# Storing the prompt's result of a convolution and S5 step by token phase: 64 outermost rows in place of 2

## The chip, the cores and the metric

The kernel runs on one core of one Trainium2 chip. The metric is the device time of one execution in microseconds (us), and of several runs the median. Before the change three runs took 2135.16, 2134.79 and 2128.93 us, median 2134.79 us.

## The reference, cut to what matters

The reference is one inference step of a two-layer trunk in float32: a short gated convolution layer and an S5 (diagonal state space) layer with a GLU, each with a residual, then a final RMSNorm. The prompt has 256 tokens, the sample batch 8, the model width is 2048 and the inner width 4096. What the change touches is the end alone: the normalised prompt rows are written out.

```python
def rmsnorm(x, g):
    xf = x.astype(jnp.float32)
    xf = xf * lax.rsqrt(jnp.mean(xf * xf, axis=-1, keepdims=True) + EPS)
    return (xf * g.astype(jnp.float32)).astype(x.dtype)
...
    y_prompt = rmsnorm(xp, final_norm)
    y_sample = rmsnorm(xs, final_norm)
```

y_prompt is 1 x 256 x 2048 float32, 2.10 MB; y_sample is 8 rows of 8 KB, 64 KB.

## The kernel before

Nearly the whole kernel is one stream of weights. SyncE (SP in the profile) loads 1 MB blocks of weights from DRAM (line 187), ScalarE and VectorE split each into two parts (lines 196 and 205), and TensorE multiplies the parts with the activations (lines 230 to 233), for the two input projections, the GLU and the two output projections in turn. The order of the work on each engine is the order in which the code records it; `Stream.go` (line 100) walks the weight blocks and puts the other work between them. All transfers of the kernel's end are issued by SP, one behind the other (`wq` is SyncE).

Tokens are kept in the order of their phase: token t = 4c + s stands at position s*64 + c, with s the phase (0 to 3) and c the chunk (0 to 63). So after the last output projection (`ssm_out`, line 1130), when results are transposed back to one token per partition, half h of the result (h = 0 or 1) has phase 2h in its partitions 0 to 63 and phase 2h + 1 in its partitions 64 to 127. The tile `o01` (a view of `yb`) holds both halves, 128 partitions x 2 x 2048.

When the weight stream has ended, the tail runs: sums of squares per token (lines 1128 and 1219 to 1222), the reciprocal root (`rstd_from`, lines 267 to 273), five scalings of pieces of `o01` (line 1229 on VectorE, line 1231 on ScalarE), and then five stores of these pieces (line 1233), in the order of the pieces, each behind a wait for the engine that scaled it. The sample's rows are scaled and stored last (lines 1234 and 1235). Line 1260 is the program's end: SP waits there for the last transfers, and the engines meet.

The view `yp` gives the result in DRAM by phase: index (phase, chunk, column), where neighbouring chunks of one phase lie four tokens apart, 32 KB. A store of half h takes two phases of it, so the access pattern in DRAM is 2 x 64 x columns, and that on the chip is 128 partitions x columns.

Each transfer that SP issues signals its landing on one of eight semaphores, which are used in turn; a transfer waits before its issue until the one eight places earlier, which had the same semaphore, has landed, unless something else has shown that already.

Of the kernel before, what the change touches and what calls it, by code (L numbers as in the profile page):

```python
# [23 lines left out]
NCH = 64  # L24
NP = LC * NCH
T = NP + NS
# [12 lines left out]


class Stream:
    """Slots of the weight stream, and what is issued between them: processes that yield a wait in slots (int), a wait
    for the time of a transfer (Lag) or the vector time they have taken (float). Side processes share a budget of vector
    time per slot."""

    def __init__(self):
        self.slots, self.now, self.t = [], 0, 0.0
# [28 lines left out]
                        again = True  # L76

    def fill(self, fn):
        """Independent vector work, issued where a chain of dependent instructions would wait, or at the slot's end."""
        self.fills.append(fn)  # L80

    def pop_fill(self):
# [42 lines left out]
def tile_hybrid_conv_s5_step(  # L125
# [7 lines left out]
    PE, V, A, P = nc.tensor, nc.vector, nc.scalar, nc.gpsimd  # L133
    mult, add, sub = ALU.mult, ALU.add, ALU.subtract
    wq, mq = nc.sync, nc.sync
# [3 lines left out]
    psm = ctx.enter_context(tc.tile_pool(name="psm", bufs=4, space=PSUM))  # L139
    pss = ctx.enter_context(tc.tile_pool(name="pss", bufs=2, space=PSUM))  # L140

# [1 line left out]
    ident = const.tile([128, 128], F32, name="ident")  # L143
    make_identity(nc, ident)
    ones = const.tile([128, 128], F32, name="ones")
# [19 lines left out]
    cp_d = dram.tile([128, G, GS], F32, name="cp_d")  # L165
    h0_d = dram.tile([128, NS, G], F32, name="h0_d")

# [1 line left out]
    wraw = ctx.enter_context(tc.tile_pool(name="wraw", bufs=3))  # L169
    wsp = ctx.enter_context(tc.tile_pool(name="wsp", bufs=4))  # L170
    s0p = ctx.enter_context(tc.tile_pool(name="s0p", bufs=1))
# [1 line left out]
    run = Stream()  # L173
    spawn, side = run.spawn, run.side

# [1 line left out]
    raws, whs, wls = {}, {}, {}  # L177

    def load_raw(i, parts=1, between=lambda: None):
# [116 lines left out]
    cs = cc.tile([128, KI, NS], F32, name="cs")  # L296
    wk = enter("convwk", 2)

    # ================= tokens to feature-major =================
    # token order s*64 + c for t = 4c + s, then the samples  # L300
    st_p = tc.tile_pool(name="start", bufs=1)
    sp = st_p.__enter__()
    xin = [sp.tile([128, D], F32, name=f"xin{i}") for i in range(2)]
# [87 lines left out]
        st_p.__exit__(None, None, None)  # L391
        second_stage()

    # ================= conv layer =================
    yHL = [None, None]
    tabs = {}

# [23 lines left out]
        side(finish(state_layout(pr)))  # L421

    def tables(pr):
        """Per-state factors of the S5 recurrence: powers of lam_bar, and those times (lam_bar - 1) / lam."""
        lamT, Ft, dcol, msk, eye = (tabs[k] for k in ("lam", "F", "dcol", "msk", "eye"))
        nt = lambda name: pr.tile([128, 2, SD], F32, name=name)
        ar, ai = nt("ar"), nt("ai")
# [121 lines left out]
            yield from cmul(fr[k], fi[k], fr[0], fi[0], lr[k], li[k])  # L549

        def spread(re, im, dst):
            """[A | B] over the states: A = re on both halves, B = -im on re rows and im on im rows."""
            w = pr.tile([128, 2, 2, 4, 2, 16], F32, name="spr")
            for half, a in enumerate((re, im)):
                av = a.rearrange("g a (pb pi) -> g (a pb) pi", pi=16)
                wv = w[:, half].rearrange("g a pb c pi -> g (a pb) c pi")
                A.activation(wv[:, :, 0, :], av, AF.Copy, scale=1.0 if half == 0 else -1.0)
                A.activation(wv[:, :, 1, :], av, AF.Copy)
            yield 1
            ps = pss.tile([128, 512], F32, name="ps_a")  # L560
            wf = w.rearrange("g f a pb c pi -> g (f a) (pb c pi)")
            for i in range(4):
                PE.transpose(ps[:, i * 128:(i + 1) * 128], wf[:, i, :], ident)
            yield 1
            A.activation(dst, ps.rearrange("p (f g) -> p f g", f=2), AF.Copy)

        for k in range(1, 5):
            yield from spread(lr[k], li[k], lamT[:, :, k - 1, :])
        P.tensor_copy(lam1, lamT[:, :, 0, :])
        P.tensor_copy(lam4, lamT[:, :, 3, :])  # L570
        for k in range(4):
            yield from spread(fr[k], fi[k], Ft[:, :, 3 - k, :])

    def state_layout(pr):
        """B, conj(C) and the samples' states with the states on the partitions."""
        for which, (re, im, dst) in enumerate(((b_re, b_im, bp_d), (c_re, c_im, cp_d))):
            for a2 in range(2):
                bo = pr.tile([128, 128, GS], F32, name="bo")
                bn = [pr.tile([128, 1024], F32, name=f"bn{c}") for c in range(2)]
                for c, src in enumerate((re, im)):  # L580
                    mq.dma_start(bn[c], src[0, a2 * 128:(a2 + 1) * 128].rearrange("g x y -> g (x y)"))
                yield 2
                pat = "g (pb pi h) -> g h pb pi" if which == 0 else "g (h pb pi) -> g h pb pi"
                for hq in range(4):
                    bw = pr.tile([128, 4, 4, 2, 16], F32, name="bw", bufs=2)
                    for c in range(2):
                        A.activation(bw[:, :, :, c, :], bn[c].rearrange(pat, pb=4, h=GS)[:, hq * 4:hq * 4 + 4], AF.Copy,
                                     scale=-1.0 if which == 1 and c == 1 else 1.0)
                    yield 1
                    ps = pss.tile([128, 512], F32, name="ps_b")  # L590
                    for h in range(4):
                        PE.transpose(ps[:, h * 128:(h + 1) * 128], bw[:, h].rearrange("g pb c pi -> g (pb c pi)"), ident)
                    yield 1
                    A.activation(bo[:, :, hq * 4:hq * 4 + 4].rearrange("p g h -> p h g"),
                                 ps.rearrange("p (h g) -> p h g", h=4), AF.Copy)
                yield 1
                mq.dma_start(dst[:, a2 * 128:(a2 + 1) * 128, :], bo)
        for a2 in range(2):
            ho = pr.tile([128, NS, 128], F32, name="bo")
            hn = [pr.tile([128, NS, SD], F32, name=f"bn{c}") for c in range(2)]  # L600
            for c, src in enumerate((state_re, state_im)):
                mq.dma_start(hn[c], src[0, :, a2 * 128:(a2 + 1) * 128, :].rearrange("b g p -> g b p"))
            yield 2
            for bq in range(2):
                hw = pr.tile([128, 4, 4, 2, 16], F32, name="bw", bufs=2)
                for c in range(2):
                    A.activation(hw.rearrange("g b pb c pi -> g (b pb) c pi")[:, :, c, :],
                                 hn[c][:, bq * 4:bq * 4 + 4, :].rearrange("g b (pb pi) -> g (b pb) pi", pi=16), AF.Copy)
                yield 1
                ps = pss.tile([128, 512], F32, name="ps_b")  # L610
                for b in range(4):
                    PE.transpose(ps[:, b * 128:(b + 1) * 128], hw[:, b].rearrange("g pb c pi -> g (pb c pi)"), ident)
                yield 1
                A.activation(ho[:, bq * 4:bq * 4 + 4, :].rearrange("p b g -> p (b g)"), ps, AF.Copy)
            yield 1
            mq.dma_start(h0_d[:, :, a2 * 128:(a2 + 1) * 128], ho)

    def table_chunks(ck):
        """V (chunk inputs), Y (outputs of a chunk's first state) and T (within a chunk) of 8 groups at a time."""
        lamT, Ft, dcol, msk, eye = (tabs[k] for k in ("lam", "F", "dcol", "msk", "eye"))  # L620
        full = [128, 8, LC, GS]

        def by_rows(d, t):
            """Rows (group, s, h) of a pair's table to rows (s, group, h)."""
            dv = d.rearrange("(s g h) q n -> g s h (q n)", s=LC, g=2)
            for g in range(2):
                mq.dma_start(dv[g], t[g * 64:g * 64 + 64])
# [33 lines left out]
        for j in range(KI):  # L661
# [26 lines left out]
            Y = ck.tile([128, 8, 5, GS], F32, name="Y", bufs=2)  # L688
# [116 lines left out]
    for jp in range(KD // 2):  # L805
        a = len(run.slots)
# [2 lines left out]
            run.at(a + 3 + m, res, 2 * jp + m)  # L809
    run.at(n_conv_in + 5, lambda: conv_states())  # L810

    # ================= S5 layer =================
    NB = G // GB
    TB = GB // 8
    NSL = 83
# [24 lines left out]
        side(scan_proc())  # L840

    def pair_rows(i):
        """Tiles 2i, 2i+1 of the token scratch as [(group, h), pair, token]."""
        return u_d[2 * i:2 * i + 2].rearrange("j (jl x) t -> x (j jl) t", x=2 * GS)

    def by_group(dst, src):
        """Both groups of each pair, each with zeros on the other's rows."""
        for g in range(2):
            A.activation(dst[:, :, g, :], src, AF.Copy, scale=gmask[:, g:g + 1])

# [207 lines left out]
        for jp in range(KI // 2):  # L1058
            group(ssm_w_in[0], half * DI + jp * 256, jp, 2, xgH, xgL, done)

    # ================= GLU =================
    bH, bL = (lambda kt: s0[:, kt, :]), (lambda kt: ss["L"][:, kt, :])

    g_split = [0]
# [39 lines left out]
    for kqs in (range(3), range(3, 4)):  # L1104
        for jp in range(PRE):
            a = len(run.slots)
# [10 lines left out]
    for jp in range(PRE, KI // 2):  # L1117
        a = len(run.slots)
# [1 line left out]
        for m in range(2):  # L1120
            run.at(a + 2 + m, glu_in, 2 * jp + m)

    # ================= output projection and final norm =================
    outs = {}

    def token_sums(a, c):
# [47 lines left out]
    for jp in range(KD // 2):  # L1174
        a = len(run.slots)
# [5 lines left out]
                for m in range(2):  # L1181
                    run.at(a + 2 * kq - 2 + m, split_out, range(kq * 8 + m * 4, kq * 8 + m * 4 + 4))

# [1 line left out]
    n_ssm, n_glu = n_conv_in + 64, n_conv_in + 64 + 128  # L1185
    U_LAG, Y_ST, Y_LD, T_BUFS = 8.0, 11.0, 10.0, 2
    V_MASK, T_MASK, Y_POOL = 1, 1, 5
# [21 lines left out]
    tiles = [(lambda kt=kt: x_tile(kt)) for kt in range(8, KD)]  # L1209
# [14 lines left out]
    yp = y_prompt.rearrange("o (c s) d -> (o s) c d", s=LC)  # L1224
    o01, osm = outs["p"], outs["s"]
# [4 lines left out]
        else:  # L1230
            A.activation(o01[:, h, cols], o01[:, h, cols], AF.Copy, scale=rt[:, h:h + 1])
    for h, c0, c1 in ((0, 0, 512), (0, 512, 1024), (0, 1024, 2048), (1, 0, 1024), (1, 1024, 2048)):
        wq.dma_start(yp[2 * h:2 * h + 2, :, c0:c1], o01[:, h, c0:c1])
    V.tensor_scalar(osm, osm, rt[:NS, 2:3], None, op0=mult)  # L1234
    wq.dma_start(y_sample.rearrange("b o d -> (b o) d"), osm)
_INS = ["x_prompt", "x_sample", "state_conv", "state_ssm_re", "state_ssm_im",
# [27 lines left out]
```

## Time and profile before

| what | us |
|---|---|
| median of three runs | 2134.79 |
| fastest and slowest run | 2128.93 and 2135.16 |
| span of the profiled execution, first to last instruction | 2129.0 |
| TensorE busy | 2047.2 (96% of the span) |
| from the issue of the first prompt store to the end of the span (2084.7 to 2129.0) | 44.3 |

For the profiled execution the profile has the span alone, with no time of its own beside it; it lies 0.1 us above the fastest run and 5.8 us under the median. Of the page, the table of 40 slices is where to begin: TensorE is busy by nine tenths or more in nearly all of them, and in the last slice by one tenth. That slice holds the tail, which the rows below show in detail.

### The profile page before, as it was taken

How to read it: one execution, taken by the hardware profiler on the slowest of the kernel's cores; microseconds unless marked ns; L12 is line 12 of the kernel's file. 1: busy time of each engine (PE TensorE's matmuls, PEld its weight loads, DVE VectorE, ACT ScalarE, POOL GpSimd, SP SyncE). 2: the span in 40 equal slices, each digit the busy share in tenths (PEclk: the TensorE clock that was granted, in tenths of full speed). 3: DMA queues.
4: the chain of work that ended last, by engine and by line, in shares of the span. 5: the costliest groups of instructions: out<-in, count | busy, mean ns of one | idle time of the engine just before them, and what ended most of it. 6: DMA issues, size and time to landing. Idle time of an engine off the chain costs nothing. (4 is left out here: it accounts for less than half of the span.)

```text
span 2129.0 us, 43518 instructions
## 1 busy us (share of the span) xinstructions
PE 2047.2 (96%) x17284; PEld 2020.2 (95%) x17284; DVE 1455.0 (68%) x3628; ACT 998.9 (47%) x1477; POOL 66.6 (3%) x161
## 2 busy tenths in 40 slices
PE   8999999999999999999899999899999999999991
PEld 7999999999999999999899989899999999999991
DVE  6785558888888888545459988798555555574441
ACT  6457554444444444444455455544654444464431
POOL 0000000000000000000000021211200000000000
PEclk9999999999999999999999999999999999999995
DMA  7666777777777777766888788979865666566541
GB/s 230 203 191 223 224 231 210 208 212 225 214 217 214 222 218 209 226 202 199 234 226 233 218 226 238 242 208 264 221 204 184 198 193 194 188 189 191 186 135 41
DMA packets 496217, 441.28 MB, mean 207 GB/s; under 512 B 110468, under 2 KB 478582, under 8 KB 495478
## 3 DMA queue, kind: packets, MB, share of 16 engines
q1 hardware_dynamic: 491886, 432.01, 68.8%
q0 software_dynamic: 4096, 6.50, 1.1%
q8 instruction: 135, 2.21, 0.4%
q14 instruction: 68, 0.56, 0.1%
q10 hardware_dynamic: 32, 0.01, 0.0%
HBM read 391.42 MB, written 47.15 MB: 206 GB/s over the span
## 5 line engine op out<-in xcount | busy, mean ns | idle before, releaser
L230 PE MATMUL acc_ps<-s,wh 128*128 128x264 f32 x4544 | 1315.1, 289 | 2.6 <-ACT sg L1096 1.8
L233 PE MATMUL acc_ps<-s,wl 128*128 128x264 f32 x4528 | 1289.4, 285 | 0.7 <-DVE wl L205 0.7
L196 ACT ACTIVATE wh<-raw 128x1024 fp32r<-128x1024 f32 x640 | 677.9, 1060 | 881.1 <-PE acc_ps L231 673.9
L205 DVE TENSOR_TENSOR wl<-raw,wh 128x1024 fp32r<-128x1024 f32 (+1 forms) x768 | 798.4, 1043 | 421.4 <-PE acc_ps L233 259.9
L231 PE MATMUL acc_ps<-s,wh 128*128 128x264 f32 x3072 | 876.4, 285 | 0.0
L230 PEld LDWEIGHTS acc_ps<-s,wh 128*128 128x128 f32 x4544 | 862.2, 190 | 11.4 <-issue 5.4
L233 PEld LDWEIGHTS acc_ps<-s,wl 128*128 128x128 f32 x4528 | 855.3, 189 | 1.1 <-DVE wl L205 1.1
L231 PEld LDWEIGHTS acc_ps<-s,wh 128*128 128x128 f32 x3072 | 584.4, 190 | 0.0
L231 PE MATMUL acc_ps<-l,wh 128*128 128x264 f32 x1472 | 418.8, 284 | 0.1
L231 PEld LDWEIGHTS acc_ps<-l,wh 128*128 128x128 f32 x1472 | 278.1, 189 | 0.3 <-DVE l L259 0.3
L230 PE MATMUL acc_ps<-yb,wh 128*128 128x264 f32 x256 | 73.0, 285 | 0.0
L230 PE MATMUL acc_ps<-ya,wh 128*128 128x264 f32 x256 | 72.9, 285 | 0.0
L231 PE MATMUL acc_ps<-yb,wh 128*128 128x264 f32 x256 | 72.8, 284 | 0.0
L233 PE MATMUL acc_ps<-ya,wl 128*128 128x264 f32 x256 | 72.7, 284 | 0.0
L233 PE MATMUL acc_ps<-yb,wl 128*128 128x264 f32 x256 | 72.7, 284 | 0.0
L231 PE MATMUL acc_ps<-ya,wh 128*128 128x264 f32 x256 | 72.6, 284 | 0.0
L902 PE MATMUL ps_a<-ub,vt 128*128 128x144 f32 x256 | 41.2, 309 | 21.1 <-DMA vt<-vt_d 19.7
L944 DVE TENSOR_TENSOR S<-S,prod 128x64 f32<-128x64 f32 x252 | 56.1, 223 | 5.3
L939 DVE TENSOR_TENSOR prod<-S,lam 128x64 f32<-128x64 f32 x252 | 56.0, 222 | 4.9
L902 PEld LDWEIGHTS ps_a<-ub,vt 128*128 128x128 f32 x256 | 36.6, 206 | 22.6 <-issue 11.4
L940 DVE STREAM_SHUFFLE S<-S 128x64 f32<-128x64 f32 x252 | 56.5, 224 | 0.0
L942 DVE TENSOR_TENSOR prod<-S,lam 128x64 f32<-128x64 f32 x252 | 55.5, 220 | 0.0
(311 smaller groups left out, 1731.0 us busy)
## 6 DMA issues: line engine op xcount, KB each, us to landing
raw<-in_conv_w_in_dram SPq DMA_DIRECT2D x127, 1024.0 KB
raw<-in_ssm_w_in_dram SPq DMA_DIRECT2D x64, 1024.0 KB
raw<-in_ssm_w_glu_dram SPq DMA_DIRECT2D x64, 1024.0 KB
raw<-in_conv_w_out_dram SPq DMA_DIRECT2D x32, 1024.0 KB
raw<-in_ssm_w_out_dram SPq DMA_DIRECT2D x32, 1024.0 KB
yt_d<-Y SPq DMA_DIRECT2D x32, 256.0 KB
vt_d<-vt SPq DMA_DIRECT2D x64, 128.0 KB
vt<-vt_d SPq DMA_DIRECT2D x16, 512.0 KB
```

The costliest lines, as they stand in the source:

```text
L196: A.activation(whs[i], raws[i][:, :, m * 128:(m + 1) * 128], AF.Copy)
L205: run.fill(lambda k=k: V.tensor_tensor(wls[i][:, k], raws[i][:, k, m * 128:(m + 1) * 128], whs[i][:, k], op=sub))
L230: PE.matmul(ps, wh[:, k, :], H(kt), start=first, stop=False)
L231: PE.matmul(ps, wh[:, k, :], L(kt), start=False, stop=False)
L233: PE.matmul(ps, wl[:, k, :], H(kt), start=False, stop=last)
L902: PE.matmul(ps[:, k * 2 * CB:(k + 1) * 2 * CB], vt[:, jj, 2 * h + k, :], ub[:, jj * 4 + 2 * h + k].rearrange("p a c -> p (a c)"), start=Tr ...
L939: V.tensor_tensor(pr[:, 0], S[:, cur, :], a4[:, 0], op=mult)
L940: V.stream_shuffle(S[:, sh, :], S[:, cur, :], SWAP)
L942: V.tensor_tensor(pr[:, 1], S[:, sh, :], a4[:, 1], op=mult)
L944: V.tensor_tensor(S[:, nxt, :], S[:, nxt, :], pr[:, 1], op=add)
```

## The change

Each of the five stores of line 1233 becomes two, one per phase s, written as a loop. Every store then takes 64 partitions, and its pattern in DRAM is 64 x columns. The number of bytes, the pieces, their order and all work ahead of the stores stay. The diff also blanks comments and docstrings, which are no instructions, and moves the lines behind the store by one (1234 and 1235 become 1235 and 1236).

```diff
     for h, c0, c1 in ((0, 0, 512), (0, 512, 1024), (0, 1024, 2048), (1, 0, 1024), (1, 1024, 2048)):
-        wq.dma_start(yp[2 * h:2 * h + 2, :, c0:c1], o01[:, h, c0:c1])
+        for s in range(2):
+            wq.dma_start(yp[2 * h + s, :, c0:c1], o01[s * NCH:(s + 1) * NCH, h, c0:c1])
     V.tensor_scalar(osm, osm, rt[:NS, 2:3], None, op0=mult)
     wq.dma_start(y_sample.rearrange("b o d -> (b o) d"), osm)
```

On SP at the end of the program, before the change: the last load of the stream, the five prompt stores (line 1233), the sample's store and the program's end. In brackets stands what an instruction waits for; DMAHW0 to DMAHW7 are the eight semaphores of SP's transfers, and the first store signals on number 1.

```order
L792 DMA yt<-x_d 128x264 [waits DMAHW4_49,DVE_49]
L1233 DMA out_dram<-yb_12700 2x64x512 [waits DVE_49] x2
L1233 DMA out_dram<-yb_12700 2x64x1024 [waits DMAHW3_49,Activation_49]
L1233 DMA out_dram<-yb_12700 2x64x1024 [waits DVE_49]
L1233 DMA out_dram<-yb_12700 2x64x1024 [waits DMAHW5_49,Activation_49]
L1235 DMA out_dram<-yb_12700 8x2048 [waits DMAHW6_49,DVE_49]
L1260 UNCONDITIONAL_BRANCH
```

The same place of SP after the change:

```order
L1234 DMA out_dram<-yb_12700 64x512 [waits DVE_49]
L1234 DMA out_dram<-yb_12700 64x512
L1234 DMA out_dram<-yb_12700 64x512 [waits DMAHW3_49,DVE_49]
L1234 DMA out_dram<-yb_12700 64x512
L1234 DMA out_dram<-yb_12700 64x1024 [waits DMAHW5_49,Activation_49]
L1234 DMA out_dram<-yb_12700 64x1024 [waits DMAHW6_49]
L1234 DMA out_dram<-yb_12700 64x1024 [waits DMAHW7_49,DVE_49]
L1234 DMA out_dram<-yb_12700 64x1024 [waits DMAHW0_49]
L1234 DMA out_dram<-yb_12700 64x1024 [waits DMAHW1_49,Activation_49]
L1234 DMA out_dram<-yb_12700 64x1024 [waits DMAHW2_49]
L1236 DMA out_dram<-yb_12700 8x2048 [waits DMAHW3_49,DVE_49]
L1261 UNCONDITIONAL_BRANCH
```

Six transfers have become eleven, none has moved past other work, and the instructions of all other engines stand as they stood. The ninth and the tenth prompt store and the sample's store (the last three transfers) now wait on semaphores 1, 2 and 3 for the landing of the first, second and third prompt store; the waits on the numbers 3, 5, 6, 7 and 0 ahead of them are for loads of the stream.

## Rows read from the trace of the kernel before

**Rows 1.** Busy time by window at the end; behind TensorE's clock DMA share and GB/s.

```profile
core 0: us, PE busy (x) PEld busy (x) DVE busy (x) ACT busy (x) POOL busy (x), PEclk, DMA share, GB/s
2075.00:2079.80 4.80, 4.80 (x42) 4.80 (x41) 1.22 (x3) 1.91 (x3) 0.00 (x0) 1.00 0.00 0
2079.80:2084.70 4.90, 2.05 (x19) 1.58 (x17) 2.68 (x14) 1.89 (x7) 0.00 (x0) 0.89 0.00 0
2084.70:2086.00 1.30, 0.00 (x0) 0.00 (x0) 1.30 (x4) 1.30 (x2) 0.00 (x0) 0.50 0.01 3
2086.00:2127.70 41.70, 0.00 (x0) 0.00 (x0) 0.94 (x1) 0.46 (x1) 0.00 (x0) 0.50 0.14 52
2127.70:2129.00 1.30, 0.00 (x0) 0.00 (x0) 0.00 (x0) 0.00 (x0) 0.00 (x0) 0.50 0.00 0
```

**Rows 2.** SP's instructions in order of time: start us, duration us, line.

```profile
2084.73 0.57 SPq L1233 DMA_DIRECT2D out_dram<-yb  x1
2085.35 0.54 SPq L1233 DMA_DIRECT2D out_dram<-yb  x1
2085.99 3.83 SPq L1233 DMA_DIRECT2D out_dram<-yb  x1
...
2094.74 9.50 SPq L1233 DMA_DIRECT2D out_dram<-yb  x1
2104.34 9.68 SPq L1235 DMA_DIRECT2D out_dram<-yb  x1
```

**Rows 3.** DMA view of 2084 to 2129: total, then issues with count and size.

```profile
DMA packets 666, 2.16 MB, mean 48 GB/s; under 512 B 18, under 2 KB 18, under 8 KB 658
...
out_dram<-yb SPq DMA_DIRECT2D x3, 512.0 KB
out_dram<-yb SPq DMA_DIRECT2D x2, 256.0 KB
out_dram<-yb SPq DMA_DIRECT2D x1, 64.0 KB
```

**Rows 4.** Waits of SP from 2075 on: us in total, times, longest.

```profile
SPq L1260 <- DMA out_dram<-yb: 13.5, 3, 9.9
```

**Rows 5.** VectorE and ScalarE in the tail, in order of time.

```profile
2084.21 1.55 DVE L1229 TENSOR_SCALAR yb<-yb,rt 128x512 f32<-128x512 f32 x3
2084.27 2.19 ACT L1231 ACTIVATE yb<-yb,rt 128x1024 f32<-128x1024 f32 x2 [1.09 <-DVE rt L273]
...
2085.67 1.27 DVE L1234 TENSOR_SCALAR yb<-yb,rt 8x2048 f32<-8x2048 f32 x1
```

**Rows 6.** The tail's transfers by window, columns as in rows 1.

```profile
2086.00:2090.00 4.00, 0.00 (x0) 0.00 (x0) 0.94 (x1) 0.46 (x1) 0.00 (x0) 0.50 0.13 34
2090.00:2114.00 24.00, 0.00 (x0) 0.00 (x0) 0.00 (x0) 0.00 (x0) 0.00 (x0) 0.50 0.13 52
2114.00:2115.00 1.00, 0.00 (x0) 0.00 (x0) 0.00 (x0) 0.00 (x0) 0.00 (x0) 0.50 0.49 102
2115.00:2127.00 12.00, 0.00 (x0) 0.00 (x0) 0.00 (x0) 0.00 (x0) 0.00 (x0) 0.50 0.13 53
```

**Rows 7.** SP near the start: sixteen stores of 128 rows, and what follows.

```profile
40.31 11.23 SPq L379 DMA_DIRECT2D x_d<-xT  x16
...
51.09 0.45 SPq L379 DMA_DIRECT2D x_d<-xT  x1
51.64 0.39 SPq L187 DMA_DIRECT2D raw<-in_conv_w_in_dram  x1
53.31 0.38 SPq L428 DMA_DIRECT2D ar<-in_ssm_a_re_dram  x1
...
SPq L379 <- DMA raw<-in_conv_w_in_dram: 2.8, 1, 2.8
...
SPq L428 <- DMA x_d<-xT: 1.0, 3, 0.4
```

**Rows 8.** Loads and stores near the start by window, columns as in rows 1.

```profile
3.00:4.00 1.00, 0.26 (x1) 0.18 (x1) 0.00 (x0) 0.00 (x0) 0.00 (x0) 1.00 1.03 372
...
40.30:51.60 11.30, 11.30 (x96) 11.30 (x95) 9.96 (x20) 4.30 (x10) 0.00 (x0) 1.00 0.90 272
```

**Rows 9.** Issue times on SP of single lines: ns min/median/max.

```profile
L187 SPq DMA_DIRECT2D raw<-in_ssm_w_out_dram x32: 367/368/383, 1868.9 to 2055.5; - x32
L983 SPq DMA_DIRECT2D out_dram<-so x16: 595/614/2112, 1220.2 to 1553.6; - x16
L766 SPq DMA_DIRECT2D out_dram<-ue x1: 3600/3600/3600, 840.9 to 840.9; - x1
```

## The prediction

> **What bounds the kernel now.** I began with the page's table of 40 slices: TensorE is full until the last slice, so only the tail can answer to a change that touches nothing but the last stores. The windows at the end show the tail [rows 1]. The matrix products end at about 2079.8 us. From there to 2084.7 the norm is worked out, a chain of small steps that the change leaves alone. From 2084.7 to 2129.0, 44.3 us or 2.1% of the span, the kernel writes its result, and for 41.7 us of that no engine has more than a moment's work: the reader is to see a DMA share of 0.14 at 52 GB/s. A share of 1 would be the core's 16 DMA engines all busy; 0.13, the share in the calm stretches [rows 6], is 2.1 engines.
>
> SP's own row tells the same from the issuing side [rows 2]. The first two stores take 0.57 and 0.54 us to issue and follow each other by 0.62 us. The third holds SP for 3.83 us, the fifth for 9.50, and the sample's small store for 9.68. A store of the same kind can't cost 0.54 and 9.50 us to issue, and a store of 64 KB still less 9.68; so SP is held because what it issued earlier has not gone out. At the end SP waits 13.5 us more for landings [rows 4]. VectorE and ScalarE are no part of that: the last piece of the prompt is scaled at 2084.27 + 2.19 = 2086.46, the sample's rows at 2086.94 [rows 5].
>
> So the end is set by 2.16 MB [rows 3] going out through two engines, at 52 / 2 = 26 GB/s each. Why two: the stores have an outermost dimension of 2 in DRAM. The sample's store, with 8 outermost rows, lifts the share to 0.49 and the rate to 102 GB/s in the one slice in which it starts to move [rows 6], and loads and stores with 128 outermost rows reach shares of 1.03 and 0.90 at 372 and 272 GB/s [rows 8]. The number of engines follows the outermost count; no row has a store of 64 rows by itself.
>
> **The change part by part.** The first issue stays at 2084.73, since nothing ahead of it moves.
>
> *Issue.* Eleven transfers stand in SP's row in place of six. The two issues that were not held follow each other by 0.62 us [rows 2]; the sixteen 128-row stores near the start take 11.23 / 16 = 0.70 us each, gaps and one wait for a load in it [rows 7]; 64-partition stores in the middle of the kernel have a median of 0.61 us [rows 9]. From below the bound is a weight load's issue, 0.37 us and some 0.05 of gap, thus 0.42 [rows 9]; from above I take 1.0, between the stores' median and their longest of 2.1 us, which lay beside the weight stream. I take 0.64, near the tail's own rows. The eleventh transfer is then issued ten steps on, at 2084.73 + 6.4 = 2091.1 (2088.9 to 2094.7).
>
> *Data.* With sixteen engines at 26 GB/s the rate would be 416 GB/s; the loads show 372, the sixteen stores 272 while a weight load shared the engines [rows 8]. The first bytes moved 1.3 us after the first issue [rows 1], so at 2086.0. The 2.16 MB then take 5.2 us at 416 and 7.9 us at 272: finished at 2091.2 to 2093.9 if SP kept up. At 340, between the two, it is 6.4 us and 2092.4, which is about where the last issue with its own first-byte time ends (2091.1 + 1.3 = 2092.4). Issue and data are nearly equal bounds, so a wrong guess of one moves the end little.
>
> *Waits.* The order of instructions adds three: the ninth, the tenth and the eleventh transfer wait for the landing of the first, second and third store. Behind them on SP stands nothing but the rest of these stores and the end. They are reached at 2084.73 + 8 x 0.64 = 2089.9 and later, 5.1 us after the store they wait for. What shows that this is long enough is the run of sixteen stores near the start: it has the same distance of eight, and the list of SP's waits has, for that line, one wait for a weight load and none for a store [rows 7], at 0.70 us a step, so 5.6 us. The last of them was issued at 51.09, and the instruction that waited for it went on at 53.31: 2.2 us from issue to landing. The first store here is 128 KB, like those. Cost nothing; if that cover were gone and a store needed 6 us, the ninth would come 0.9 us late.
>
> *Scaled pieces.* With SP no longer held, the stores come to the scaled pieces earlier. The fifth and sixth need the piece that ScalarE ends at about 2085.4, and are reached at 2087.3; the ninth needs the one that ends at 2086.46 [rows 5] and is reached at 2089.9. Nothing waits here.
>
> *The end.* From the last issue at 2091.1, the landing comes 2.2 us on by the row of the sixteen stores, at 2093.3, and 1.3 us lie between the last byte and the end of the span [rows 1]: 2094.6. By the other way, first byte at 2092.4, 0.3 us for 64 KB on eight engines at 26 GB/s, and 1.3 us, it is 2094.0. I take 2094.2. From both sides: 2091.2 + 1.3 = 2092.5 with the quickest issue and 416 GB/s; 2094.7 + 1.3 + 0.3 + 1.3 = 2097.6 with the slowest issue. A gain of 2129.0 - 2094.2 = **34.8 us**, between 31.4 and 36.5. No later work is waiting to become the last: the products end at 2079.8, and the norm's chain is where it was.
>
> *What the skill says of it.* The Trainium skill, page DMA: Bandwidth & Descriptors, section Rules for kernel authors, speaks against this change: of two transfers to disjoint halves of the partitions it says not to bother, as both halves go over all the DMA engines anyway and serialize, and one transfer of 128 partitions is better. By the rows its premise does not hold here, since the store of 128 partitions stands at a share of 0.13 and not near 1. By that rule the sum would be no gain, the second rival below; by the rows it is 34.8 us. The same page, section Why a DMA increments its semaphore by 16 and not by 1, has the number of engines as the largest up to 16 that divides the slowest dimension of both sides, which gives 2 before and 16 after; for 64 rows no row here can show it.
>
> **The rivals.** First, *the engines open up but something else takes half of it.* The mechanism is SP's issue: one store from 64 partitions in the middle of the kernel held SP for 3.60 us, another for 2.11 [rows 9]. At 2.1 us each the last issue comes at 2084.73 + 21 = 2105.7 and the end at 2108.8 to 2109.2, a gain of 20 us and a time near 2115. For it: the two rows, and that the first 4 us of the stores ran at 34 GB/s and not 52 [rows 6], so something beside the engine's pace can slow a store. Against it: both rows lay amid the weight stream, where a transfer is held by what is queued ahead, and the tail has nothing queued.
>
> Second, *the halves share the same two engines.* Then 2.16 MB leave at 52 GB/s as before, and the five added issues at 0.62 us hide in the 41.7 us in which the engines work through the bytes, or at most add 3.1 us: 2134.8 to 2137.9. For it: no 64-row store stands alone in the trace. Against it: the share of 0.49 for eight rows and 0.90 and more for 128.
>
> Third, *slower: each store falls to one engine.* The split store is a flat list of 64 rows in place of 2 x 64. If the engines were given out by pieces of a higher dimension and not by rows, a store would have one piece, and 2.10 MB at 26 GB/s would take 81 us, 40 us more than now: about 2175. It decides from the point at which a store gets fewer than two engines. For it: the outermost count of 2 could be read that way. Against it: the sixteen stores are flat lists of 128 rows, and had a share of 0.90.
>
> **How the numbers follow.** The gain is made against the span of 2129.0. The runs lie between 2128.93 and 2135.16, so that the profiled execution belongs to the quickest of them; the tail's length does not hang on what makes the others 6 us longer, and I take the gain from the median: 2134.79 - 34.8 = 2100.0 us. About 0.3%, 6.4 us, is what a measurement of this kernel can tell from no change.
>
> Chances: the forecast 0.87; half taken away 0.08; no change 0.03; slower 0.02. The range goes from the quickest run less the largest gain, 2128.93 - 36.5 = 2092.4, to the slowest less the smallest, 2135.16 - 31.4 = 2103.8: 2092 to 2104, which is the forecast's own case with its bounds and leaves out the rivals' 0.13. Faster by over 0.3%: 0.87 + 0.08 = 0.95; within: 0.03; slower: 0.02.
>
> **What would show it.** In the profile after, the DMA share between the first store and the end should be near 0.9 at 300 GB/s or more, for 6 to 8 us in place of 41.7. SP's stores should take 0.5 to 0.7 us each, with none held for several us. SP's waits should list no store waiting for a store by more than 1 us, and the last wait for a landing should be 2 to 3 us, not 13.5. The span should end 9 to 13 us after the first store's issue. The prediction is wrong if the share stays at 0.13 (second rival), falls to 0.06 (third), or if SP's issues grow to 2 us while the share stays low (first).

## The result, and the profile after

The changed kernel takes 2096.39 us (median of four runs, 2093.87 to 2102.23), the kernel before 2131.86 us (four runs, 2126.95 to 2135.16). The ratio is 0.9853 with a 95% interval of 0.9833 to 0.9874: 1.5% faster, 35.5 us between the medians. Forecast were 2100.0 us and a gain of 34.8.

The gain is best read in the tail, from the issue of the first prompt store to the end of the span: 44.3 us before, 2100.5 - 2088.5 = 12.0 us after. SP's queue at the end, instruction by instruction (start us, duration us, line), to be held against [rows 2]:

```profile
2088.47 0.49 SPq L1234 DMA_DIRECT2D out_dram<-yb  x1
2089.01 0.59 SPq L1234 DMA_DIRECT2D out_dram<-yb  x1
...
2090.99 0.55 SPq L1234 DMA_DIRECT2D out_dram<-yb  x1
...
2092.28 0.60 SPq L1234 DMA_DIRECT2D out_dram<-yb  x1
2092.92 0.96 SPq L1234 DMA_DIRECT2D out_dram<-yb  x1
2093.98 0.71 SPq L1234 DMA_DIRECT2D out_dram<-yb  x1
2094.73 1.11 SPq L1234 DMA_DIRECT2D out_dram<-yb  x1
2095.94 0.58 SPq L1236 DMA_DIRECT2D out_dram<-yb  x1
```

No store holds SP for more than 1.11 us, where the third, the fifth and the sample's had held it for 3.83, 9.50 and 9.68. SP's waits from there on, against [rows 4]:

```profile
SPq L1261 <- DMA out_dram<-yb: 2.5, 4, 1.0
SPq L1261 <- PEq L1261: 0.7, 2, 0.5
```

SP's last waits for landings take 2.5 us together and not 13.5, and no store waits for a store. The tail's windows (the last three columns are TensorE's clock, the DMA share and GB/s), against [rows 1, 6]:

```profile
2088.50:2089.60 1.10, 0.00 (x0) 0.00 (x0) 1.10 (x3) 1.10 (x2) 0.00 (x0) 0.50 0.00 0
2089.60:2092.30 2.70, 0.00 (x0) 0.00 (x0) 1.08 (x1) 0.60 (x1) 0.00 (x0) 0.50 0.90 209
2092.30:2098.90 6.60, 0.00 (x0) 0.00 (x0) 0.00 (x0) 0.00 (x0) 0.00 (x0) 0.50 0.81 242
2098.90:2100.50 1.60, 0.00 (x0) 0.00 (x0) 0.00 (x0) 0.00 (x0) 0.00 (x0) 0.50 0.00 0
```

The share rose from 0.13 to 0.8 and 0.9, so the other engines came in. But the rate is 209 and 242 GB/s, together 233 over 9.3 us, where 416 would be eight times the old one. Divided by the engines that are busy (share x 16), that is 14.5 and 18.7 GB/s an engine, against 25 before (52 GB/s at 0.13): the engines are busy, each at six to eight tenths of its old pace.

The number of engines can also be counted. [rows 3] had 18 packets under 512 B, and no row's piece of a store here is that small; the tail after the change has 168:

```profile
DMA packets 816, 2.16 MB, mean 173 GB/s; under 512 B 168, under 2 KB 168, under 8 KB 808
```

One such packet for each engine that a store uses gives 5 x 2 + 8 = 18 before and 10 x 16 + 8 = 168 after, where the 8 are the sample's. So the split stores run on sixteen engines each. The kernels below bear this count out, with other numbers of engines.

The span fell by 28.5 us only, since this execution reached its first store 3.7 us later than that of the kernel before (2088.47 against 2084.73). That need not be the change's: in another execution of the same kernel, below, the first store is issued at 2082.20.

### The profile page after: what moved, and what is told of

It is laid out like the page before. It is cut to its first block, busy times and chain, and to the rows that moved or that the text cites. A ratio compares the mean times of both kernels' runs of the same rounds, so it can differ in the third digit from the quotient of the medians.

```text
span 2100.5 us, 43525 instructions
## 1 busy us (share of the span) xinstructions
PE 2047.9 (97%) x17284; PEld 2020.1 (96%) x17284; DVE 1455.0 (69%) x3628; ACT 999.4 (48%) x1477; POOL 66.8 (3%) x161
```

## The experiments

The theory: the outermost count of a store sets on how many engines it runs. The rival: what helped is that there are ten smaller stores in place of five. The edits below are to the changed kernel where nothing else is said. "Tail" is always from the first prompt store's issue to the end of the span, in one profile of each kernel.

**Ten stores without the split by phase.**

```diff
-        for s in range(2):
-            wq.dma_start(yp[2 * h + s, :, c0:c1], o01[s * NCH:(s + 1) * NCH, h, c0:c1])
+        for d in range(2):
+            cd = slice(c0 + d * (c1 - c0) // 2, c0 + (d + 1) * (c1 - c0) // 2)
+            wq.dma_start(yp[2 * h:2 * h + 2, :, cd], o01[:, h, cd])
```

> Ten prompt stores as in the changed kernel, of the same sizes, but split by columns: each keeps the pattern of 2 x 64 x columns. Theory (the outermost count sets how many DMA engines work on a store): the share stays at 0.13 and 52 GB/s, the tail from the first store's issue to the end stays at 43 to 46 us, the time near 2131. Rival (what helped is that there are ten smaller stores in place of five): a share near 0.8 and a tail near 12 us, the time near 2096.

It took 2129.01 us in one run, beside 2129.05 for the kernel before on that chip. The tail is 2127.2 - 2081.66 = 45.5 us; the middle of it:

```profile
2083.00:2126.00 43.00, 0.00 (x0) 0.00 (x0) 0.87 (x1) 0.39 (x1) 0.00 (x0) 0.50 0.14 50
```

The same number of stores of the same sizes gives nothing as long as the outermost count is 2. The small packets number 28 = 10 x 2 + 8, two engines to a store. The rival falls.

**Row counts that sixteen doesn't divide.** Each 64-row store is cut in two, at row 62, 57 or 61:

```diff
-            wq.dma_start(yp[2 * h + s, :, c0:c1], o01[s * NCH:(s + 1) * NCH, h, c0:c1])
+            for a, b in ((0, 62), (62, 64)):
+                wq.dma_start(yp[2 * h + s, a:b, c0:c1], o01[s * NCH + a:s * NCH + b, h, c0:c1])
```

> Each 64-row store of the changed kernel is cut into 62 rows and 2 rows, twenty prompt stores in all. Theory (the engines are the largest number up to 16 that divides the outermost count): 62 and 2 both go to two engines, 2.16 MB at 52 GB/s is 41.5 us, a tail of 43 to 45 us, time near 2131. Rival (any store with 16 or more outermost rows goes over all sixteen): a share of 0.8 or more, and a tail that twenty-one issues of 0.62 us set, 13 + 4.5 = 17 to 18 us, time near 2102.

> As the store in 62 and 2 rows, but 57 and 7. Theory (largest divisor up to 16): 57 = 3 x 19 goes to three engines and 7 to seven: 1.87 MB at 78 GB/s is 24 us, the small stores add about 1 us on the same engines, a share near 0.2 and a tail of 27 to 29 us, time near 2115. Rival (a power of two, or one engine for any odd count): 57 rows on one engine, 72 us, a tail of 75 us.

> As the store in 62 and 2 rows, but 61 and 3. Theory (largest divisor up to 16): 61 is prime, so 61 rows go to one engine: 2.0 MB at 26 GB/s is 77 us, a share of 0.06 to 0.07, a tail near 80 us, time near 2165, slower than the kernel before by about 35 us. This is the slower rival of the prediction, brought about on purpose. Rival (sixteen engines for any count of 16 or more): a tail of 17 to 18 us, time near 2102.

The times were 2129.68, 2113.55 and 2165.97 us, one run each, and the tails 45.1, 30.6 and 81.8 us. The windows within the tails, for 62, 57 and 61 rows:

```profile
2084.00:2126.00 42.00, 0.00 (x0) 0.00 (x0) 1.02 (x1) 0.54 (x1) 0.00 (x0) 0.50 0.14 51
```

```profile
2083.00:2110.00 27.00, 0.00 (x0) 0.00 (x0) 0.37 (x1) 0.00 (x0) 0.00 (x0) 0.50 0.27 78
```

```profile
2084.00:2150.00 66.00, 0.00 (x0) 0.00 (x0) 0.61 (x1) 0.13 (x1) 0.00 (x0) 0.50 0.07 27
```

At 26 GB/s an engine, 51 and 78 GB/s are two and three, and 27 is one. The share of 0.27 with 57 rows would be 4.3 engines, so there the rate alone doesn't settle the number. The small packets do, here for 57 and for 61 rows:

```profile
DMA packets 757, 2.17 MB, mean 25 GB/s; under 512 B 108, under 2 KB 108, under 8 KB 748
```

```profile
DMA packets 697, 2.17 MB, mean 25 GB/s; under 512 B 48, under 2 KB 48, under 8 KB 688
```

108 is 10 x 3 + 10 x 7 + 8, so three engines for 57 rows and seven for the 7 rows beside them; 48 is 10 x 1 + 10 x 3 + 8 with 61 and 3 rows, and with 62 and 2 rows, where it is 48 too, 10 x 2 + 10 x 2 + 8. So 62 rows (2 x 31) run on two engines, 57 (3 x 19) on three and 61, a prime, on one: the largest number up to 16 that divides the rows. Taking three of 64 rows out of a store turned a gain of 35 us into a loss of 37 (2165.97 against 2129.05). That is the prediction's slower rival at its point of decision, fewer than two engines, where it had put the loss at 40 us; what brings it about is the divisor of the row count, and not pieces of a higher dimension as the rival had it.

With 57 rows the tail came out 2 us over the expected 29. Here the wait that the order of instructions had shown, a transfer's on the one eight places before it, did show up (with 62 rows it came to 1.1 us in all). Whether it makes these 2 us was not tried:

```profile
SPq L1235 <- DMA out_dram<-yb: 9.4, 6, 2.5
...
SPq L1237 <- DMA out_dram<-yb: 2.5, 1, 2.5
```

With 64 rows it never did: there a store lands before its semaphore's turn comes.

**What holds the rate at 233 GB/s: issue, piece size, or the step in DRAM?** Three kernels. First, twice as many stores, each of 32 rows:

```diff
-            wq.dma_start(yp[2 * h + s, :, c0:c1], o01[s * NCH:(s + 1) * NCH, h, c0:c1])
+            for a in (0, 32):
+                wq.dma_start(yp[2 * h + s, a:a + 32, c0:c1], o01[s * NCH + a:s * NCH + a + 32, h, c0:c1])
```

> Each 64-row store of the changed kernel is cut into two of 32 rows: twenty prompt stores, twenty-one transfers, the same bytes. If SP's issue is a bound near that of the data, as the prediction's sum has it: the last issue comes 20 x 0.62 = 12.4 us after the first, the tail is 15 to 17 us. If the data alone set the pace (240 GB/s): the tail stays at 12 to 13 us. The wait of each transfer on the one eight places before it now spans 5 us or so of issue for stores of 64 to 128 KB, and should cost nothing.

The time is 2096.40 us in one run, the tail 2094.6 - 2081.80 = 12.8 us, not the 15 to 17 expected if issue sets it. SP's line for it (ns min/median/max), the start of its last transfer, and the windows:

```profile
L1235 SPq DMA_DIRECT2D out_dram<-yb x20: 350/422/457, 2081.8 to 2090.6; - x20
2091.20 0.29 SPq L1237 DMA_DIRECT2D out_dram<-yb  x1
2083.00:2086.30 3.30, 0.00 (x0) 0.00 (x0) 1.01 (x1) 0.53 (x1) 0.00 (x0) 0.50 0.55 139
2086.30:2092.50 6.20, 0.00 (x0) 0.00 (x0) 0.00 (x0) 0.00 (x0) 0.00 (x0) 0.50 0.93 261
```

These stores take 0.42 us to issue and not 0.62, so that twenty-one go out in 9.7 us, one every 0.47. The expectation for issue was built on the wrong price, and issue is not out of the picture: while the pieces are 2 KB, 64 KB every 0.47 us is 139 GB/s, which is what moved, at a share of 0.55. In the changed kernel the first four stores, 128 KB each, are issued 0.63 us apart (2088.47 to 2090.99 for four), which is 208 GB/s, so issue alone would also give the 209 there. With the 4 KB pieces it is the data that set the pace: 256 KB every 0.63 us would be 416 GB/s, 242 moved, the last byte came 3.0 us after the last issue, and the issues of 0.7 to 1.1 us are best read as SP being held by the data, as before, for less long.

Second, the first two pieces stored together, so that all pieces are 4 KB:

```diff
-    for h, c0, c1 in ((0, 0, 512), (0, 512, 1024), (0, 1024, 2048), (1, 0, 1024), (1, 1024, 2048)):
+    for h, c0, c1 in ((0, 0, 1024), (0, 1024, 2048), (1, 0, 1024), (1, 1024, 2048)):
```

> The changed kernel with its first two pieces of 512 columns stored together: eight prompt stores, all with pieces of 4 KB, nine transfers in place of eleven. If the 2 KB pieces are what held the first microseconds of the changed kernel's stores to about 200 GB/s: the rate is 300 or more throughout, 2.16 MB in 7 us, and the tail from the first issue 10 us. If the writes or the 32 KB step hold it: still 240 GB/s, 9 us of data, a tail of 11.5 to 12 us. In both cases the first store starts 0.4 us later, as it needs both scaled pieces. Time within 2 us of the changed kernel, 1.5 to 1.8% under the kernel before.

2098.17 us, 0.985 of the kernel before (0.983 to 0.9871); tail 11.2 us:

```profile
2087.90:2091.00 3.10, 0.00 (x0) 0.00 (x0) 0.68 (x1) 0.20 (x1) 0.00 (x0) 0.50 0.95 252
2091.00:2096.50 5.50, 0.00 (x0) 0.00 (x0) 0.00 (x0) 0.00 (x0) 0.00 (x0) 0.50 0.76 251
```

252 GB/s against 233. Piece size, and with it the issue of 2 KB pieces, plays a small part; it isn't what keeps the rate from 416.

Third, the result brought to token order. The last layer's sum (line 1141) is written with its columns in the order of tokens, for one more VectorE instruction of 8 columns on each tile of the result; then a half of the result is 128 neighbouring tokens, and five stores of 128 rows do:

```diff
-        V.tensor_tensor(x2, ps, xrs.pop(n), op=add)
+        xr = xrs.pop(n)
+        V.tensor_tensor(x2[:, NP:], ps[:, NP:], xr[:, NP:], op=add)
+        by_token = lambda a: a[:, :NP].rearrange("p (s c) -> p c s", s=LC)
+        V.tensor_tensor(x2[:, :NP].rearrange("p (c s) -> p c s", s=LC), by_token(ps), by_token(xr), op=add)
...
-        for s in range(2):
-            wq.dma_start(yp[2 * h + s, :, c0:c1], o01[s * NCH:(s + 1) * NCH, h, c0:c1])
+        wq.dma_start(y_prompt[0, h * 128:(h + 1) * 128, c0:c1], o01[:, h, c0:c1])
```

> The last layer's sum is written in token order, so that a half of the result has 128 tokens in a row and its five stores go to 128 neighbouring rows in DRAM: outermost count 128, six transfers in place of eleven, pieces of a store 8 KB apart in DRAM and not 32 KB. Theory (sixteen engines for 128 as for 64): share 0.8 or more, no store held for long, a tail of 12 us or less, faster than the kernel before by 1.4 to 1.8%. On what held the changed kernel's data to 240 GB/s: if the eleven issues or the 32 KB step did, the rate goes to 340 or more and the tail to 8.5 to 9.5 us; if the pieces of 2 KB or the writes themselves do, it stays near 240 and the tail at 11.5 to 12.

2090.77 us, 0.9821 of the kernel before (0.9798 to 0.9843). The tail is 2089.6 - 2081.0 = 8.6 us:

```profile
2080.90:2082.10 1.20, 0.00 (x0) 0.00 (x0) 1.20 (x4) 1.20 (x2) 0.00 (x0) 0.50 0.24 92
2082.10:2084.00 1.90, 0.00 (x0) 0.00 (x0) 1.07 (x1) 0.59 (x1) 0.00 (x0) 0.50 1.05 382
2084.00:2088.20 4.20, 0.00 (x0) 0.00 (x0) 0.00 (x0) 0.00 (x0) 0.00 (x0) 0.50 0.87 316
2088.20:2089.60 1.40, 0.00 (x0) 0.00 (x0) 0.00 (x0) 0.00 (x0) 0.00 (x0) 0.50 0.00 0
```

Its first stores, in 2 KB pieces, run at 382 GB/s where the changed kernel's ran at 209. Three things differ: the number of issues (six in place of eleven, and each shorter, 0.34 to 0.42 us where nothing held it), and two that my expectation had not kept apart, the rows' step in DRAM (8 KB in place of 32 KB) and the partitions that one store reads (128 in place of 64). The next two kernels tell these two apart.

**Half the partitions, or the step in DRAM?** The token-order kernel with each store cut into two of 64 partitions:

```diff
-        wq.dma_start(y_prompt[0, h * 128:(h + 1) * 128, c0:c1], o01[:, h, c0:c1])
+        for s in range(2):
+            wq.dma_start(y_prompt[0, h * 128 + s * 64:h * 128 + s * 64 + 64, c0:c1], o01[s * 64:s * 64 + 64, h, c0:c1])
```

> The token-order kernel with each of its five stores cut into two of 64 partitions: eleven transfers as in the changed kernel, but neighbouring rows in DRAM, 8 KB apart and not 32 KB. Theory (a store from 64 partitions reads half of the on-chip memory's ways out, so that sixteen engines share them and run at half pace): the first microseconds stay near 209 GB/s as in the changed kernel, the whole near 235, and the tail near 12 us. Rival (the 32 KB step of the rows in DRAM held the changed kernel): 340 GB/s or more and a tail of 9 to 10 us, set by eleven issues.

And the changed kernel with the second half's stores on ScalarE's queue:

```diff
-            wq.dma_start(yp[2 * h + s, :, c0:c1], o01[s * NCH:(s + 1) * NCH, h, c0:c1])
+            (wq if s == 0 else A).dma_start(yp[2 * h + s, :, c0:c1], o01[s * NCH:(s + 1) * NCH, h, c0:c1])
```

> The changed kernel with the stores of the second half of the partitions issued by ScalarE's own DMA queue, those of the first half and the sample's by SP: the same ten stores with the same rows in DRAM, but both halves of the partitions can be read at once. ScalarE issues its first store only after its two scalings, so 1.9 us after SP's first. Theory (half of the ways out per store): once both queues run, 340 GB/s or more, 2.16 MB in 7 to 7.5 us with the slower first 2 us, a tail of 9.5 to 10.5 us. Rival (the 32 KB step in DRAM holds the rate): 235 GB/s and 12 us as in the changed kernel, less at most the 1 us that SP's longer issues cost.

The first took 2097.02 us, 0.9857 of the kernel before (0.9839 to 0.9874), with a tail of 2091.5 - 2079.68 = 11.8 us:

```profile
2081.00:2083.70 2.70, 0.00 (x0) 0.00 (x0) 0.89 (x1) 0.41 (x1) 0.00 (x0) 0.50 0.90 210
2083.70:2090.10 6.40, 0.00 (x0) 0.00 (x0) 0.00 (x0) 0.00 (x0) 0.00 (x0) 0.50 0.80 244
```

With neighbouring rows, but 64 partitions to a store, it is the changed kernel again, 210 and 244 GB/s against 209 and 242. The step in DRAM, 8 or 32 KB, makes no difference that shows. Against the token-order kernel it has eleven issues again as well as half the partitions, but issue does not explain the pace: the share is 0.90 and not the 0.55 of the thirty-two-row stores, and an engine that is busy moves 210 / (16 x 0.90) = 14.6 GB/s, where it moved 382 / (16 x 1.05) = 22.7 with 128 partitions.

The second took 2096.17 us, 0.9843 (0.9828 to 0.9858), with a tail of 2092.8 - 2082.16 = 10.6 us:

```profile
2083.40:2089.10 5.70, 0.00 (x0) 0.00 (x0) 0.97 (x1) 0.49 (x1) 0.00 (x0) 0.50 0.98 321
2089.10:2091.40 2.30, 0.00 (x0) 0.00 (x0) 0.00 (x0) 0.00 (x0) 0.00 (x0) 0.50 0.44 137
```

The same stores with the 32 KB step run at 321 GB/s for 5.7 us, 20.5 for an engine that is busy, when both halves of the partitions can be read at once; then the last of them run out at 137. That is a little under the 340 GB/s expected, and the whole time shows no gain over the changed kernel. ScalarE's stores did not start 1.9 us late, as I had expected, but together with SP's, at 2082.16 in the profile.

So the pace of a busy engine goes with the partitions that are being read at one time: 14.5 and 14.6 GB/s in the first windows with stores of 64 on one queue, 20.5 with both halves on two queues, 22.7 from stores of 128. (In the later windows with stores of 64 it is 18.7 and 19.1; why these are quicker was not tried.) One rival stands: two queues also issue twice as fast, and no kernel here has two queues that both read the same half. Against it is that one queue is enough for 22.7 with stores of 128, and that the thirty-two-row stores' busy engines moved only 139 / (16 x 0.55) = 15.8 GB/s although much of the time they had nothing to do, so that they were slow without being crowded.

The Trainium skill, page SBUF — State Buffer, section Door 1: The DMA port swizzle, states such a rule: partitions 0 to 63 reach 8 of 16 ports, and it gives about 218 GB/s as the limit for them. The 209 and 210 here lie near it, but do not test it, since issue alone gives 208 there; which partition has which port no run here shows.

**The changed kernel again,** beside the others:

> The changed kernel as it is, beside the others on the same chip: a tail of 12 us from the first store to the end, 1.3 to 1.7% under the kernel before. It tells whether the 3.7 us by which its profiled execution reached the tail later belong to the change: if they do, the first store is issued near 2088.5 again; if they are a matter of the single execution, it lies anywhere from 2081 to 2089, as the times of the kernel before spread over 8 us.

2095.86 us, 0.9839 (0.9818 to 0.986), tail 2094.0 - 2082.20 = 11.8 us:

```profile
2082.20 7.38 SPq L1234 DMA_DIRECT2D out_dram<-yb  x10
2089.67 0.70 SPq L1236 DMA_DIRECT2D out_dram<-yb  x1
```

Its first store comes 6.3 us sooner than in the first profile of the same kernel. What makes executions differ by that much ahead of the tail was not tried.

The token-order kernel has the shortest tail of all, 3.2 us under this one's. In whole times the intervals of the two (0.9798 to 0.9843 and 0.9818 to 0.986) overlap, so it is the tail of one profile that shows it, beside 12.0 and 11.8 in the two of the changed kernel.

## Why the prediction was right, and where not

**What bounds the tail: right.** Two engines because the outermost count is 2. Ten stores that keep the 2 stay at 50 GB/s, and 62, 57 and 61 rows move at the pace of two, three and one. The Trainium skill's rule on the number of engines (page DMA: Bandwidth & Descriptors, section Why a DMA increments its semaphore by 16 and not by 1), which the prediction had put beside the sum and no row could show, agrees at each of these counts.

**The sum: the mechanism right, the data's term mis-sized.** Forecast were 9.5 us from the first issue to the end, 12.0 were measured, within the 9 to 13 that the prediction gave for it. By terms: issue of eleven transfers, 6.4 forecast and 2095.94 - 2088.47 = 7.5 measured; first byte after 1.3 forecast, 1.1 measured; the data, 6.4 us at 340 GB/s forecast, 9.3 us at 233 measured; after the last byte 1.3 forecast, 1.6 measured. The step that failed is the rate: I took it between the loads' 372 and the sixteen stores' 272 [rows 8], all from transfers with 128 partitions, and the changed stores read 64. The lower bound of 272 was no bound, and of the prediction's signs two did not come, 300 GB/s or more and 6 to 8 us of data. The tail still came out inside the range because I had left room for issues of 1.0 us, which was the wrong reason: that part was luck.

**"Issue and data are nearly equal bounds": right for the first four stores alone.** There issue gives 208 GB/s and 209 moved. Over the whole tail the data were the longer, with 9.3 us and an end 3.0 us after the last issue; ten issues more made the tail 0.8 to 1.0 us longer, so issue is not far behind.

**The waits: right.** None of the three new waits cost anything, as the row of sixteen stores had it [rows 7]; that they can was seen with 57 rows.

**The Trainium skill's rule against the change** (page DMA: Bandwidth & Descriptors, section Rules for kernel authors). It would have given no gain, and the gain was 35.5 us; the premise, that the one transfer already uses all engines, was what failed, as the share of 0.13 had said. But its advice, one transfer from 128 partitions in place of two halves, holds once sixteen engines can serve that transfer: 8.6 us against 11.8 for the same rows in halves. That halves serialize, as the rule has it, is not what their stores on two queues show, 321 GB/s and 10.6 us. The prediction had set the rule aside whole and not asked what the halves themselves cost.

**The rivals.** Half the gain lost to SP's issue: it did not happen, the longest issue was 1.11 us. By its own terms that rival's earlier end is 2105.7 + 2.9 = 2108.6, not 2108.8, which changes nothing. No change: only where stores stayed on two engines, with the 2 kept and with 62 rows. Slower: not with 64 rows, but with 61.

**The time.** Between the medians the gain is 35.5 us and in the tail 32.3. The other 3 us can lie in the scatter of the executions, which is 6 us at the first store's issue for one and the same kernel; beside the second series of the kernel before the gain is 33.4 us, with 44.3 - 11.8 = 32.5 in the tail. That the forecast of 34.8 came near 35.5 therefore says little of the sum; the tail does. A slip of mine bears on it too: I set the span of 2129.0 beside the fastest run's time, but a run's time is 1.7 to 1.8 us longer than its span wherever both are on record (2102.23 and 2100.5 here). By that, an estimate, the profiled execution before stands near 2130.8, in the middle of the runs and not with the quickest.

## What to carry to other kernels

When the last thing a kernel does is to store its result, look at the DMA share there: a low and constant one with nothing else running means few engines, and the outermost count of the access pattern is the place to look. Make that count a multiple of 16 (64 rows took the tail from 44.3 to 12.0 us, 61 rows made it 81.8), and then let one store read all 128 partitions, which took the tail to 8.6 us here for another order of the result further up.

## What the runs showed of the hardware that I had not expected

Sixteen engines that store from 64 partitions on one queue move 209 to 252 GB/s in the windows shown, and from 128 partitions 316 to 382; two queues, each with one half of the partitions, reach 321. The step between rows in DRAM, 8 or 32 KB, made no difference. The number of engines that stores use can be counted in the packets under 512 B of the DMA view: one for each engine and store makes up the count in every run here. The issue of a store on SP has no fixed price, and fewer rows don't make it cheaper: 0.42 us in the median for 32 rows, 0.5 to 0.6 for 64 and 0.34 to 0.42 for 128 in token order where nothing held it, and up to 9.7 us where the engines had not yet taken what was issued before.
